# Other SBUF addresses for split weights and activations in a two-block transformer kernel on one core

## The chip, the core and the metric

One core of a Trainium2 chip runs the whole program. The metric is device time in microseconds of one execution. TensorE multiplies, VectorE and ScalarE do the elementwise work, and transfers from HBM are issued by SyncE's queue (SP). GpSimd sets a few tiles to zero.

## The reference

Two blocks follow each other on x of 256 tokens by 1,024 channels, all in float32. The first has two layers, each of a SwiGLU (1,024 to 2 x 2,816 to 1,024), a mixer and a second SwiGLU, with RMS norms and residuals around each; the mixer is a short convolution in the first layer and a gated delta rule with 16 heads in the second. The second block has sparse attention and an RWKV-7 recurrence side by side, merged by gates, and then a feed-forward with a convolution of width 3.

```python
def swiglu(x, w_gate_up, w_down):
    gate, up = jnp.split(x @ w_gate_up, 2, axis=-1)
    return (jax.nn.silu(gate) * up) @ w_down
...
for i in range(DEPTH):
    ff = swiglu(rms_norm(h, g[0]), ffn_w_gate_up[i, 0], ffn_w_down[i, 0])
    h = h + 0.5 * rms_norm(ff, g[1])
    ...  # mixer: h = h + rms_norm(mix, g[3])
    ff = swiglu(rms_norm(h, g[4]), ffn_w_gate_up[i, 1], ffn_w_down[i, 1])
    h = h + 0.5 * rms_norm(ff, g[5])
```

Nearly all the work lies in 19 products of x, or of a hidden activation, with a weight matrix (the list SEQUENCE).

## The kernel before

**Products in three terms.** Activations lie transposed, 128 channels on the partitions by 256 tokens, and a product takes weight tiles of 128 x 128 as TensorE's stationary operand. Both operands are split into a high part in TensorE's rounded format (fp32r) and the low part that remains. Each tile then takes three matmuls of 256 columns: high weight with high x, high weight with low x, low weight with high x (`mm3`, and `mm3s` for a product's first slices).

**The weight stream.** All weights lie in HBM as one stream of chunks, each of 128 partitions by four tiles (2,048 bytes to a partition). A chunk is loaded to one of six tiles wraw; ScalarE rounds it into one of seven tiles whi, VectorE subtracts that from wraw into one of seven tiles wlo (`split_next`), and the two are used for four tiles in turn (`next`). In the gated delta rule's input product a part of the chunks is split into a region arG instead (`borrow`).

**Operands.** The products up, sc_in, gdn_in, rw, nsa, merge, out2 and cup read the tiles xh and xl: the normed x, eight slices of 256 tokens. The products down, sc_out, gdn_out, proj and cdown read hidden activations in the regions a0, a1 and a2: slot k (of 256 columns) of these three in a row holds the high part of slice k, slot 22 + k its low part (`hidden`). The regions hold matrices of the two mixers in between. The profile writes whi, wlo, wraw and a for all buffers of a kind. In time, the products stand as up, down, sc_in, sc_out, up, down, up, down, gdn_in, gdn_out, up, down, rw, nsa, merge, proj, out2, cup, cdown; the third and fourth up run from about 470 and 920 us, and cup and cdown end the program.

**Addresses.** One pool places the tiles in the order in which they are made, each at the next multiple of 32 bytes of the partition. `fill` tiles hold nothing; they only move what follows. Worked out from the sizes, the tiles of the chunked products start at these remainders by 512 bytes; all slices and weight tiles within them are 512 or 1,024 bytes apart, so they keep the remainder:

| tile | before | changed |
|---|---|---|
| xh | 0 | 0 |
| xl | 0 | 16 |
| whi, seven buffers | 64 each | 32, 64, 96, 128, 160, 192, 224 |
| wlo, seven buffers | 64 each | 256, 288, 320, 352, 384, 416, 448 |
| a0 | 128 | 32 |
| a1 | 128 | 40 |
| a2 | 128 | 104 |
| arG | 128 | 128 |
| arM, fg, rb, acc, tmp, stm, x0 | 0 | 32 |

**The order of the work.** The program is made twice. In the first pass every instruction is recorded as a node with its engine, a price and what it depends on; a list scheduler (`ranks`, `schedule`) then sets an order for each engine, and the second pass issues the same instructions with that order (`arrange`). Dependences are kept by grains of 64 columns of a tile, counted from the tile's start:

```python
GRAIN = 64
...
cols = np.unique(cols // self.GRAIN).tolist()
```

Six times, at the start of a product whose x is made from the product before, `prepare` makes eight slices of h, xh and xl on VectorE and ScalarE while TensorE begins with slice 0.

Of the kernel before, what the change touches and what calls it, by code (L numbers as in the profile page):

```python
# [11 lines left out]
F32 = mybir.dt.float32  # L12
F32R = mybir.dt.float32r
# [6 lines left out]
P = 128  # L20
D = 1024
T = 256
KD = D // P
# [23 lines left out]
class Product:  # L47
# [4 lines left out]
    def __init__(self, name, index, kt, cols, groups=(), rows=None):  # L52
        rows = rows or [[(k * P, P)] for k in range(kt)]
        self.kt = kt
        self.cols = [c if isinstance(c, tuple) else (name, index, c, rows) for c in cols]
        self.groups = list(groups) + [1] * (len(cols) - sum(groups))
        self.order = []
        c = 0
        for n in self.groups:
            self.order += [(k, c + i) for k in range(kt) for i in range(n)]  # L60
            c += n
# [198 lines left out]
class Pace:  # L260
# [195 lines left out]
    def node(self, engine, op, out, ins, outs, price):  # L456
# [14 lines left out]
        for ap in [*ins, *outs]:  # L471
            tag = (getattr(ap.tensor, "tag", None) or "").split("_sb")[0]
            if tag in REGIONS:
                if self.current.get(tag) != ap.tensor.name:
# [145 lines left out]
class Streamer:  # L620


    def __init__(self, K, n_raw=6, n_split=7):
        self.K = K
        self.nc = K.nc
        pool = K.pool
        self.fill0 = pool.tile([P, 16], F32, name="fill2")
        self.raw = [pool.tile([P, CT * P], F32, name=f"wraw{i}") for i in range(n_raw)]
        self.hi = [pool.tile([P, ST * P], F32R, name=f"whi{i}") for i in range(n_split)]
        self.lo = [pool.tile([P, ST * P], F32R, name=f"wlo{i}") for i in range(n_split)]  # L630
        self.fill1 = pool.tile([P, 16], F32, name="fill3")
        self.order, self.place, self.at, self.ring = list(range(N_CHUNKS)), {}, {}, 0
        self.loaded = self.split = self.pos = 0

# [57 lines left out]


FILL = 24, 32
REGIONS = {"a0": 4096, "a1": 4096, "a2": 3072, "fg": 2048, "arG": 12288}


class Kernel:
    def __init__(self, nc, pool, psum, wstream, params, consts, xt, lowrank, w1, out):
        nc = self.nc = Engines(nc)  # L700
        self.pool = pool
        self.wstream, self.out, self.lowrank, self.w1 = wstream, out, lowrank, w1
        self.banks = [psum.tile([P, 512], F32, name=f"bank{i}") for i in range(8)]
        self.bank_at = 0
        self.side_at = 0
        self.par = pool.tile([P, N_PARAM], F32, name="par")
        self.eps = pool.tile([P, 1], F32, name="eps")
        self.half = pool.tile([P, 4, KD], F32, name="half")
        self.pad = [pool.tile([P, T + 3], F32, name=f"pad{i}") for i in range(5)]
        self.fill = [pool.tile([P, FILL[0]], F32, name="fill0")]  # L710
        self.con = pool.tile([P, N_CONST], F32, name="con")
        self.fill += [pool.tile([P, FILL[1]], F32, name="fill1")]
        self.h = pool.tile([P, KD, T], F32, name="h")
        self.xh = pool.tile([P, KD, T], F32R, name="xh")
        self.xl = pool.tile([P, KD, T], F32R, name="xl")
        self.regions = {}
        self.arM = pool.tile([P, 2048], F32, name="arM")
        self.fg = self.region("fg").rearrange("p (k t) -> p k t", t=T)
        self.rb = pool.tile([P, T], F32, name="rb")
        self.rb2 = pool.tile([P, T], F32, name="rb2")  # L720
        self.acc = pool.tile([P, T], F32, name="acc")
        self.tmp = [pool.tile([P, T], F32, name=f"tmp{i}") for i in range(8)]
        self.stm = [pool.tile([P, 512], F32, name=f"stm{i}") for i in range(4)]
        for t in self.pad:
            nc.vector.memset(t[:, :3], 0.0)
        self.fg0 = self.pad[4][:, 3:]
        self.x0 = [pool.tile([P, T], F32R, name=f"x0{i}") for i in range(2)]
        self.first = None
        self.tmp_at, self.tmp_n = 0, len(self.tmp)
        self.warm()  # L730
        self.table("natural_log_exp_and_others")
        self.W = Streamer(self)
        n = PCOLS["norm_g"][1]
        nc.pace.hurry = FIRST
        self.W.load_to(1)
        nc.sync.dma_start(self.par[:, :n], params[:, :n])
        nc.sync.dma_start(self.h[:, 0, :], xt[0:P, :])
        nc.pace.hurry = 0.0
        self.W.load_to(2)
        for i, (a, b) in enumerate(((1, 2), (2, 4), (4, 8))):  # L740
            nc.sync.dma_start(self.h[:, a:b, :], xt[a * P:b * P, :].rearrange("(k p) t -> p k t", p=P))
            self.W.load_to(3 + i)
        nc.sync.dma_start(self.con, consts)
        nc.sync.dma_start(self.par[:, n:], params[:, n:])
        nc.vector.memset(self.eps, EPS)
        for i, (l, j) in enumerate(((0, 1), (0, 5), (1, 1), (1, 5))):
            nc.vector.tensor_scalar(self.half[:, i], self.gain(l, j), 0.5, None, op0=ALU.mult)
# [11 lines left out]
    def region(self, tag, dtype=F32):  # L759

        n = self.regions[tag] = self.regions.get(tag, 0) + 1
        return self.pool.tile([P, REGIONS[tag]], dtype, name=f"{tag}_{n}", tag=tag)

    def hidden(self, **kept):

# [1458 lines left out]
```

## Time and profile before

| | us |
|---|---|
| median of 2 runs | 1554.49 (1554.04 to 1554.94) |
| profiled execution | 1564.22 |
| its span, first to last instruction | 1562.0 |
| TensorE matmuls busy (13,544 records) | 1545.8 |
| TensorE weight loads busy | 1495.5 |
| VectorE busy | 1199.4 |
| ScalarE busy | 1026.1 |

The times of the views are microseconds from the span's start. Every matmul has a weight load of its own, which overlaps the matmul before it. The records of matmuls overlap too (a record of 0.28 us, one every 0.11 us), so a sum of their times, or the mean of one, does not say how fast they follow each other; their count in a window does. The granted clock is TensorE's: 1.00 is 2.4 GHz, 0.50 is 1.2 GHz. A float32 matmul that is not fp32r appears as two records.

### The profile page before, as it was taken

The numbers are of one execution on the slowest core, as the hardware profiler recorded it, in microseconds if no ns is written. First come the engines' busy times: TensorE is split into PE (matmuls) and PEld (weight loads), VectorE is DVE, ScalarE is ACT, GpSimd is POOL, SyncE is SP. The second block draws the span as 40 slices with busy tenths as digits, with TensorE's granted clock in tenths as the row PEclk, the third lists the DMA queues.
The fourth block names the chain that finished last, engine by engine and source line by source line (L and its number), as shares of the span: only waits on it lengthen the run. The fifth ranks groups of instructions, "written<-read, shape, count | busy, mean of one in ns | idle before, by whom it ended". The sixth has DMA issues, their size and how long they took to land.

```text
span 1562.0 us, 35927 instructions
## 1 busy us (share of the span) xinstructions
PE 1545.8 (99%) x13544; PEld 1495.5 (96%) x13544; DVE 1199.4 (77%) x2527; ACT 1026.1 (66%) x2153; POOL 10.4 (1%) x24
## 2 busy tenths in 40 slices
PE   9999999999999999999999999999999999999999
PEld 9999999999999999989898899999997877999999
DVE  7776597887659777689897778775788866789973
ACT  7556566765657557678787866555683666578863
POOL 0000000000000000000000000000001000000000
PEclk9999999999999999999999999999998999999999
DMA  8666656566665667525342356666533322566664
GB/s 272 198 195 190 181 182 192 168 202 194 191 185 175 195 196 248 171 82 176 115 135 83 129 155 203 185 188 189 166 113 115 98 67 84 167 189 197 195 196 123
DMA packets 142670, 261.14 MB, mean 167 GB/s; under 512 B 15904, under 2 KB 17952, under 8 KB 142368
## 3 DMA queue, kind: packets, MB, share of 16 engines
q1 hardware_dynamic: 142496, 258.84, 55.5%
q8 instruction: 106, 1.74, 0.5%
q14 instruction: 68, 0.56, 0.1%
HBM read 257.73 MB, written 1.05 MB: 166 GB/s over the span
## 4 chain that ended last, share of the span: by engine, by line
PE 95%; ACT 2%; DVE 1%; issue 0%; DMA 0%; SPq 0%; DVEq 0%; ACTq 0%
PE bank L576 95%; ACT a L576 1%; ACT stm L576 1%; DVE a L576 0%; ACT arG L576 0%; ACT whi L576 0%; DVE fg L576 0%; DVE arG L576 0%; DMA h<-xt 0%; DVE wlo L576 0%; DVE xl L576 0%; DVE pad L576 0%; DVE tmp L576 0%; ACT pad L576 0%; ACT arM L576 0%
## 5 line engine op out<-in xcount | busy, mean ns | idle before, releaser
L576 ACT ACTIVATE whi<-wraw 128x512 fp32r<-128x512 f32 x956 | 599.2, 631 | 416.9 <-PE bank L576 311.8
L576 DVE TENSOR_TENSOR wlo<-wraw,whi 128x512 fp32r<-128x512 f32 x956 | 653.5, 689 | 274.8 <-ACT whi L576 268.6
L576 PE MATMUL bank<-xh,whi 128*128 128x256 f32 x2688 | 748.7, 283 | 5.7 <-DVE stm L576 3.6
L576 PE MATMUL bank<-xh,wlo 128*128 128x256 f32 x2688 | 746.8, 282 | 0.0
L576 PE MATMUL bank<-xl,whi 128*128 128x256 f32 x2688 | 740.7, 280 | 0.7 <-DVE xl L576 0.7
L576 PEld LDWEIGHTS bank<-xh,whi 128*128 128x128 f32 x2688 | 504.7, 189 | 14.6 <-issue 6.0
L576 PEld LDWEIGHTS bank<-xl,whi 128*128 128x128 f32 x2688 | 503.7, 189 | 8.1 <-issue 5.8
L576 PEld LDWEIGHTS bank<-xh,wlo 128*128 128x128 f32 x2688 | 502.7, 189 | 6.9 <-issue 5.9
L576 PE MATMUL bank<-a,whi 128*128 128x256 f32 x2272 | 403.8, 280 | 0.2
L576 PEld LDWEIGHTS bank<-a,whi 128*128 128x128 f32 x2272 | 347.1, 188 | 1.2 <-DVE a L576 0.5
L576 PE MATMUL bank<-a,wlo 128*128 128x256 f32 x1136 | 317.4, 279 | 0.0
L576 PEld LDWEIGHTS bank<-a,wlo 128*128 128x128 f32 x1136 | 212.7, 187 | 0.0
L576 DVE TENSOR_TENSOR tmp<-bank,rb 128x256 f32<-128x256 f32 x176 | 66.4, 419 | 6.6 <-ACT rb L576 1.4
L576 ACT ACTIVATE xh<-h,par 128x256 fp32r<-128x256 f32 x70 | 34.1, 499 | 12.7 <-DVE h L576 10.6
L576 ACT ACTIVATE arG<-bank 128x256 f32<-128x256 f32 (+2 forms) x87 | 37.8, 443 | 5.8 <-PE bank L576 5.5
L576 PE MATMUL bank<-a 64*128 64x256 f32 (+3 forms) x192 | 39.5, 380 | 1.5 <-DVE arG L576 1.5
L576 ACT ACTIVATE a<-tmp 128x256 fp32r<-128x256 f32 x88 | 35.8, 407 | 7.7 <-DVE tmp L576 7.6
L576 DVE TENSOR_TENSOR acc<-acc,tmp 128x256 f32<-128x256 f32 x92 | 38.6, 419 | 2.0 <-ACT acc L576 1.0
L576 DVE SCALAR_TENSOR_TENSOR arG<-arG,par 128x256 f32<-128x256 f32 x88 | 40.0, 477 | 0.0
L576 DVE TENSOR_TENSOR a<-tmp,a 128x256 fp32r<-128x256 f32 x88 | 36.8, 418 | 3.8 <-ACT a L576 3.8
L576 ACT ACTIVATE tmp<-tmp 128x256 f32<-128x256 f32 x88 | 35.4, 407 | 3.8 <-DVE tmp L576 3.7
L576 DVE TENSOR_TENSOR tmp<-tmp,tmp 128x256 f32<-128x256 f32 x88 | 36.7, 418 | 0.0
(253 smaller groups left out, 1226.1 us busy)
## 6 DMA issues: line engine op xcount, KB each, us to landing
wraw<-wstream SPq DMA_DIRECT2D x968, 256.0 KB, 2.9
arG<-cmp_w SPq DMA_DIRECT2D x1, 1024.0 KB, 4.8
out_dram<-h SPq DMA_DIRECT2D x8, 128.0 KB, 2.8
con<-consts SPq DMA_DIRECT2D x1, 734.0 KB, 5.4
h<-xt SPq DMA_DIRECT2D x1, 512.0 KB, 6.3
a<-lowrank SPq DMA_DIRECT2D x1, 512.0 KB, 4.1
par<-params SPq DMA_DIRECT2D x1, 283.5 KB, 4.7
h<-xt SPq DMA_DIRECT2D x2, 128.0 KB, 3.2
```

Of the source, the lines that this page charges most:

```text
L576: i = f(*args, **kw)
```

## The change

Each of the fourteen buffers whi and wlo is followed by a fill tile of eight elements (32 bytes), so the next one starts 32 bytes further by 512. The tile xl is made four elements longer, and its view begins at the fourth; likewise a view of region a1 begins at element 2 and of a2 at element 10 of a longer tile. The fill tile ahead of the raw weights goes. No instruction is added or taken away, and none has other operands than before but for their addresses.

```diff
--- before.py
+++ after.py
@@ -624,11 +624,17 @@
         self.K = K
         self.nc = K.nc
         pool = K.pool
-        self.fill0 = pool.tile([P, 16], F32, name="fill2")
         self.raw = [pool.tile([P, CT * P], F32, name=f"wraw{i}") for i in range(n_raw)]
-        self.hi = [pool.tile([P, ST * P], F32R, name=f"whi{i}") for i in range(n_split)]
-        self.lo = [pool.tile([P, ST * P], F32R, name=f"wlo{i}") for i in range(n_split)]
-        self.fill1 = pool.tile([P, 16], F32, name="fill3")
+        self.fills = []
+
+        def stepped(name):
+            t = pool.tile([P, ST * P], F32R, name=name)
+            self.fills.append(pool.tile([P, 8], F32, name=name + "f"))
+            return t
+
+        self.hi = [stepped(f"whi{i}") for i in range(n_split)]
+        self.lo = [stepped(f"wlo{i}") for i in range(n_split)]
+        self.fills.append(pool.tile([P, 16], F32, name="fill3"))
         self.order, self.place, self.at, self.ring = list(range(N_CHUNKS)), {}, {}, 0
         self.loaded = self.split = self.pos = 0
 
@@ -692,6 +698,8 @@
 
 
 FILL = 24, 32
+
+SHIFT = {"a1": 2, "a2": 10}
 REGIONS = {"a0": 4096, "a1": 4096, "a2": 3072, "fg": 2048, "arG": 12288}
 
 
@@ -712,7 +720,7 @@
         self.fill += [pool.tile([P, FILL[1]], F32, name="fill1")]
         self.h = pool.tile([P, KD, T], F32, name="h")
         self.xh = pool.tile([P, KD, T], F32R, name="xh")
-        self.xl = pool.tile([P, KD, T], F32R, name="xl")
+        self.xl = pool.tile([P, KD * T + 4], F32R, name="xl")[:, 4:].rearrange("p (k t) -> p k t", t=T)
         self.regions = {}
         self.arM = pool.tile([P, 2048], F32, name="arM")
         self.fg = self.region("fg").rearrange("p (k t) -> p k t", t=T)
@@ -759,7 +767,8 @@
     def region(self, tag, dtype=F32):
 
         n = self.regions[tag] = self.regions.get(tag, 0) + 1
-        return self.pool.tile([P, REGIONS[tag]], dtype, name=f"{tag}_{n}", tag=tag)
+        at = SHIFT.get(tag, 0)
+        return self.pool.tile([P, REGIONS[tag] + at], dtype, name=f"{tag}_{n}", tag=tag)[:, at:]
 
     def hidden(self, **kept):
```

Since the planner counts grains from the tile's start, the shifted views give it other dependences, and the orders that it sets differ in places. The first piece is VectorE's, at the start of sc_in, where prepare makes h, xh and xl anew (tmp holds the normed output of the product before, fg that output, rb the norm's factor). Before:

```order
L576 TENSOR_TENSOR h<-h,tmp_94 128x256
L576 TENSOR_TENSOR tmp_88<-fg_84,rb_86 128x256
L576 TENSOR_TENSOR tmp_90<-fg_84,rb_86 128x256
L576 TENSOR_TENSOR h<-h,tmp_88 128x256
L576 SCALAR_TENSOR_TENSOR xl<-h,par,xh 128x256
L576 TENSOR_TENSOR h<-h,tmp_90 128x256
L576 TENSOR_TENSOR tmp_92<-fg_84,rb_86 128x256
L576 SCALAR_TENSOR_TENSOR xl<-h,par,xh 128x256
```

and now:

```order
L576 TENSOR_TENSOR h<-h,tmp_94 128x256
L576 TENSOR_TENSOR x_106<-tmp_92,x_105 128x256
L576 TENSOR_TENSOR tmp_88<-fg_84,rb_86 128x256
L576 TENSOR_TENSOR tmp_93<-fg_84,rb_86 128x256
L576 SCALAR_TENSOR_TENSOR xl<-h,par,xh 128x256
L576 TENSOR_TENSOR h<-h,tmp_88 128x256
L576 TENSOR_TENSOR tmp_90<-fg_84,rb_86 128x256
L576 TENSOR_TENSOR h<-h,tmp_93 128x256
L576 TENSOR_TENSOR h<-h,tmp_90 128x256
L576 TENSOR_TENSOR tmp_92<-fg_84,rb_86 128x256
L576 SCALAR_TENSOR_TENSOR xl<-h,par,xh 128x256 x3
```

Before, the two rows of xl are slices 1 and 2. Now slice 1 stands where it stood, and the row "x3" holds slices 2, 0 and 3: slice 2 has moved behind two more operations, and slice 0 has come forward.

The second piece is TensorE's, in gdn_in, where matmuls of the delta rule's decays (a_5 is region a2, con a table of constants) stand among those of the stream. Before:

```order
L576 MATMUL bank_62<-xh,whi_127 128x256
L576 MATMUL bank_62<-xl,whi_127 128x256
L576 MATMUL bank_64<-a_5_7962,con 128x512
L576 MATMUL bank_62<-xh,wlo_134 128x256
L576 MATMUL bank_61<-xh,whi_127 128x256
```

and now:

```order
L576 MATMUL bank_62<-xh,whi_129 128x256
L576 MATMUL bank_62<-xl,whi_129 128x256
L576 MATMUL bank_62<-xh,wlo_143 128x256
L576 MATMUL bank_64<-a_5_7975,con 128x512
L576 MATMUL bank_61<-xh,whi_129 128x256
```

The matmul with con has moved behind one matmul of the stream. From here to the end of the delta rule, and again in the second block's mixers, TensorE's order differs by such moves; from the start to here, in the up and down products outside the mixers, and in cup and cdown it is the same.

## Rows read from the trace of the kernel before

**Rows 1.** The page, parts 1 and 2: busy time; granted TensorE clock by fortieths.
```profile
PE 1545.8 (99%) x13544; PEld 1495.5 (96%) x13544; DVE 1199.4 (77%) x2527; ACT 1026.1 (66%) x2153; POOL 10.4 (1%) x24
...
PEclk9999999999999999999999999999998999999999
```

**Rows 2.** The page, part 4: shares of the chain that ended last.
```profile
PE 95%; ACT 2%; DVE 1%; issue 0%; DMA 0%; SPq 0%; DVEq 0%; ACTq 0%
```

**Rows 3.** Groups of matmuls, whole span: count | busy, mean of one | idle before.
```profile
L576 PE MATMUL bank<-xh,whi 128*128 128x256 f32 x2688 | 748.7, 283 | 5.7 <-DVE stm L576 3.6 <-DVE pad L576 1.4 <-ACT xh L576 0.7
L576 PE MATMUL bank<-xh,wlo 128*128 128x256 f32 x2688 | 746.8, 282 | 0.0
L576 PE MATMUL bank<-xl,whi 128*128 128x256 f32 x2688 | 740.7, 280 | 0.7 <-DVE xl L576 0.7
L576 PE MATMUL bank<-a,whi 128*128 128x256 f32 x2272 | 403.8, 280 | 0.2
L576 PE MATMUL bank<-a,wlo 128*128 128x256 f32 x1136 | 317.4, 279 | 0.0
...
L576 PE MATMUL bank<-xh,arG 128*128 128x256 f32 x96 | 17.0, 287 | 0.0
...
L576 PE MATMUL bank<-xl,arG 128*128 128x256 f32 x48 | 11.9, 284 | 0.0
```

**Rows 4.** Windows, TensorE: length, busy (records), granted clock, DMA share, GB/s.
```profile
1400.00:1480.00 80.00, 80.00 (x709) 1.00 0.66 195
950.00:1010.00 60.00, 60.00 (x512) 1.00 0.64 190
1050.00:1100.00 50.00, 50.00 (x427) 1.00 0.64 187
1500.00:1555.00 55.00, 55.00 (x469) 1.00 0.56 167
660.00:668.00 8.00, 8.00 (x70) 1.00 0.01 2
```

**Rows 5.** Groups of matmuls from 1400 to 1460.
```profile
L576 PE MATMUL bank<-xh,whi 128*128 128x256 f32 x177 | 48.9, 276 | 0.0
```

**Rows 6.** Groups of matmuls from 950 to 1010.
```profile
L576 PE MATMUL bank<-xh,whi 128*128 128x256 f32 x170 | 47.8, 281 | 0.0
```

**Rows 7.** Groups of matmuls from 1500 to 1560.
```profile
L576 PE MATMUL bank<-a,whi 128*128 128x256 f32 x333 | 58.9, 280 | 0.0
```

**Rows 8.** Timeline, TensorE, after 845: start, length of the merged run.
```profile
845.28 1.95 PE L576 MATMUL bank<-arG,a 128*128 128x128 f32 x16
```

**Rows 9.** Groups of VectorE instructions, shapes apart.
```profile
L576 DVE SCALAR_TENSOR_TENSOR arG<-arG,par 128x256 f32<-128x256 f32 x88 | 40.0, 477 | 0.0
...
L576 DVE SCALAR_TENSOR_TENSOR arG<-pad,par,arG 128x256 f32<-128x256 f32 x16 | 7.6, 478 | 0.0
```

**Rows 10.** Waits of TensorE: total us, times, longest.
```profile
PE bank L576 <- DVE stm L576: 3.6, 1, 3.6
...
PE bank L576 <- DVE xl L576: 0.7, 2, 0.5
```

**Rows 11.** Windows of the three stretches at half clock, all engines.
```profile
771.50:778.40 6.90, 5.96 (x26) 5.81 (x27) 6.90 (x22) 4.58 (x11) 0.00 (x0) 0.51 0.37 115
1191.40:1201.60 10.20, 10.20 (x38) 7.88 (x36) 5.87 (x12) 2.66 (x5) 1.11 (x2) 0.50 0.08 26
1263.10:1266.50 3.40, 3.40 (x43) 2.83 (x44) 1.90 (x5) 3.34 (x9) 0.00 (x0) 0.50 0.23 77
```

**Rows 12.** Timeline, VectorE, start of the first sc_in product.
```profile
195.25 0.48 DVE L576 SCALAR_TENSOR_TENSOR xl<-h,par,xh 128x256 fp32r<-128x256 f32 x1
...
196.32 0.48 DVE L576 SCALAR_TENSOR_TENSOR xl<-h,par,xh 128x256 fp32r<-128x256 f32 x1
```

**Rows 13.** Timeline, TensorE, the same start.
```profile
196.56 0.84 PE L576 MATMUL bank<-xl,whi 128*128 128x256 f32 x6
...
197.36 0.28 PE L576 MATMUL bank<-xl,whi 128*128 128x256 f32 x1
```

## The prediction

> **What bounds the kernel now.** I began with the busy shares, the granted clock and the chain of waits. TensorE is busy in 99% of the span, its weight loads in 96%, and 95% of the chain that ended last is TensorE's own work [rows 1, 2]; VectorE (77%) and ScalarE (66%) have room. So the time is the number of matmuls times the step from one to the next, plus little else: the longest single wait of TensorE for another engine is 3.6 us [rows 10].
>
> Then the groups of matmuls: the chunked products issue 3 x 2,688 with xh or xl as the moving operand, 2,272 + 1,136 with a region a, and 96 + 48 with weights in arG [rows 3], 11,616 together. Their mean of 280 ns is no step, since they overlap; the step is a window's length over its count. A matmul record lasts 0.28 us and a window counts every record that touches it, so I add 0.28 us to the length. Last product with xh and xl: 80.28 us / 709 = **113.2 ns**. Last product with a: 55.28 / 469 = **117.9 ns**. The down product at 1050 to 1100: 50.28 / 427 = 117.8 ns [rows 4]. All at full clock, with TensorE busy throughout, and each window holds one kind of work [rows 5, 7]. So the same instruction, 256 columns against 128 x 128 weights, has two rates 4.5 ns apart, and what differs by the code is the address: xh and xl start at remainder 0 by 512 bytes, the a regions at 128, the weights of both at 64. But the window 950 to 1010 holds xh and xl again, at the addresses of 1400 to 1460 [rows 5, 6], and steps at 60.28 / 512 = 117.7 ns [rows 4]. So the address alone doesn't set the rate; a stretch can settle in either. With arG (weights at 128, moving operand at 0) the step is 8.28 / 70 = 118.3 ns [rows 4].
>
> By these, 3,408 matmuls with a, the 8 x 44 x 3 = 1,056 of the product around 950 and the 144 with arG run slow, 7,008 fast at best; the mean step is about 115.0 ns.
>
> **The change part by part.**
>
> *Remainders of the fourteen weight buffers, and shifts of xl, a1 and a2.* No matmul is added or removed, so the term is 11,616 times whatever the step changes by. The trace never shows these remainders: bounds are its nearest rows. Upward, the arG step of 118.3 ns for everything: 7,008 x 5.1 + 4,464 x 0.5 = 38 us lost. Downward, the shortest step of 128-column weights under a 256-cycle stream: sixteen fp32 matmuls with arG and a in 1.95 us, (1.95 - 0.28) / 15 = 111.3 ns [rows 8]; 11,616 x 3.7 = 43 us gained. Those read half as many moving bytes, so I take them as an end and not as the value. In between lies the fast rate of this very work. I take: the matmuls with a go from 117.8 to 113.2 ns, since what all their windows share is the distance between their one remainder and the weights' one remainder, and after the change there is no such fixed distance; 3,408 x 4.5 = **15.3 us gained**. The product around 950 stays as it is (4.8 us more if it too turns fast), arG stays (its own tile keeps remainder 128; 0.7 us).
>
> The Trainium skill has a rule against the shifts: its page SBUF — State Buffer, section Specifications (TRN2), gives lines of 16 bytes and a penalty for each crossing. A row of 1,024 bytes at 8 modulo 16 touches 65 lines where it touched 64; as an estimate from that page, 1/64 of a step, 1.8 ns on at most 3,408 matmuls, 6 us lost. No row here has such a moving operand in the chunked products.
>
> *VectorE and ScalarE on shifted tiles.* Nothing: a SCALAR_TENSOR_TENSOR that reads a pad at an offset of a few elements takes 478 ns, one with aligned operands 477 [rows 9], and neither engine is the bound.
>
> *The planner's order.* It tracks dependences in grains of 64 elements, so a 256-element slice shifted by 4, 2 or 10 elements touches five grains and shares one with its neighbour. Hence the pieces of order shown. At the six starts where x is made anew, xl of slice 2 waits behind two more VectorE operations. Before, it began at 196.32 [rows 12] for a matmul at 197.36 [rows 13]; xl takes 0.48 us, so the slack is 0.56 us. Two operations later at 0.33 us each it is late by 0.1 us; with the semaphore 0.2 us, and six starts give **1.2 us lost**. Slice 3 has 2 us more and is in time. The weight splits put back there by the same move, nine operations or some 3 us, lie behind a ring of seven buffers of 12 matmuls each, 9.5 us; if that cover were gone, the move would cost those 3 us a start. SP's order swaps a few neighbouring loads, which the ring hides too.
>
> In the delta-rule and attention stretches some hundreds of matmuls change places with a neighbour or a few, at 0.1 us each. That can move a wait or one of three stretches at half clock: 20.5 us, in which TensorE is busy for 19.6 us [rows 11], so they cost up to 9.8 us now. If order cured them, 10 us are gained; a fourth like the longest would lose 5 us. I take 0.
>
> **Sum.** The profiled execution took 1564.2 us (span 1562.0, the rest around it); -15.3 + 1.2 = -14.1 us makes it 1550. The median of the runs is 1554.5, 0.6% less, so the forecast is 1554.5 - 14.1 = **1540 us**. With the product around 950 and arG fast too it is 1535; the order's ends take these to 1525 and 1545, and if a third of the matmuls with a stay slow, to 1550.
>
> **The rivals.**
>
> *No contention by address.* The Trainium skill, page TensorE: Matmul & The Clock Gate, section Step-by-step: what each phase is for, says that weight loads and the moving operand come through two independent ports, and that loading the next weights takes nothing from a running matmul. As a mechanism here: the two rates are only states left by what ran before, and the layout is without effect. For it: the slow product at the fast product's addresses [rows 5, 6]. Against it: the matmuls with a are slow in both windows of them [rows 4]. Time: 1554.5 + 1.2 = 1556. Chance 0.12.
>
> *Better than the fast rate.* The fast rate itself holds some interference between the two reads, and spread remainders remove it. For it: the 111.3 ns of the fp32 matmuls [rows 8]. Against it: 113.2 ns is held in both early and late products, as a floor would be. At 111.3 ns throughout, 1554.5 - 43 + 1 = 1512. The first page's back-to-back formula, N / 2.4 + 2.5, would give 109.2 ns; as an estimate, 1488. This decides (over 2% faster) once the mean step is under 112.3 ns. Chance 0.29.
>
> *Slower: the fast stretches are lost.* The products with xh and xl run fast at one fixed pair of remainders, 0 against 64. Now the pair changes every four weight tiles, half of the weight buffers start at an odd multiple of 32 bytes, xl at 16, a1 and a2 at 8, and the stream settles where arG's did. For it: arG, the one other distance in the trace, is the slowest of all, and one whole product fell slow at the good pair. Against it: nothing in the trace shows a cost of a start within 64 bytes. With all at 117.8 ns: 7,008 x 4.5 = 32 us, 1587; with all at 118.3, 1594. It decides from a mean step of 117.7 ns. Chance 0.17.
>
> **How the numbers follow.** About 2% (31 us) can be told from no change here. The forecast has 0.42, all of it within 2%, and so has the rival without effect, 0.12: same 0.54. Faster 0.29, slower 0.17. The range goes from 1500, which leaves out the third of the second rival that comes nearest to a full cure (0.09), to 1588, which leaves out the half of the last above it (0.08). The likeliest case's own range is 1525 to 1550.
>
> **What would show it.** Count over length again. Right: windows of the down products at 113 to 114 ns (some 488 matmuls in 55 us where 469 stood), xh and xl unchanged. No contention: 117.8 with a, as now. Better: any window of a chunked product under 112 ns. Slower: windows with xh and xl at 117 ns or more. The order's step is right if TensorE's waits for VectorE's xl grow to about 1 us and no more; it is wrong if the half-clock stretches change by over 5 us. The forecast is wrong if the rates within one window mix by buffer, which no row of before can show.

## The result, and the profile after

The changed kernel takes 1601.8 us (median of 2 runs, 1601.1 to 1602.5) where the kernel before took 1554.5 on the same chip: 1.028 times as long, with a 95% interval of 1.023 to 1.033. It is slower. The forecast was 1540 us, the range 1500 to 1588; both missed.

The changed kernel's profile, busy time, answers to [rows 1]:

```profile
PE 1581.5 (99%) x13544; PEld 1529.3 (96%) x13544; DVE 1202.2 (75%) x2527; ACT 1026.1 (64%) x2153; POOL 10.3 (1%) x24
```

TensorE is still busy for 99% of the span, with as many instructions as before. It is busy 35.7 us longer, and the span is 38.6 us longer (1600.6). VectorE worked 2.8 us longer, ScalarE as long as before. So the same matmuls took longer; TensorE's idle time, span less busy, only went from 16.2 to 19.1 us. (The chain of waits is no help here: walked back from the end it stops after 10% of the span.)

Its groups of matmuls, as in [rows 3] (count | busy, mean of one | idle before), say where:

```profile
L576 PE MATMUL bank<-xh,whi 128*128 128x256 f32 x2688 | 754.1, 284 | 6.2 <-DVE pad L576 2.7 <-DVE tmp L576 2.0 <-ACT xh L576 1.0
L576 PE MATMUL bank<-xh,wlo 128*128 128x256 f32 x2688 | 752.5, 284 | 0.0
L576 PE MATMUL bank<-xl,whi 128*128 128x256 f32 x2688 | 751.5, 284 | 1.0 <-DVE xl L576 1.0
L576 PE MATMUL bank<-a,whi 128*128 128x256 f32 x2272 | 409.2, 282 | 0.2
L576 PE MATMUL bank<-a,wlo 128*128 128x256 f32 x1136 | 320.5, 282 | 0.0
```

Every group is busy 3 to 11 us longer, and the idle times hardly differ. Since the records overlap, the steps have to come from windows. These answer to [rows 4] (length, TensorE busy and records, granted clock, DMA share, GB/s): two windows with xh and xl, the second in the product that ran slow before, the last down product with a, and the stretch with arG:

```profile
40.00:120.00 80.00, 80.00 (x681) 1.00 0.66 188
...
980.00:1040.00 60.00, 60.00 (x512) 1.00 0.66 190
...
1540.00:1595.00 55.00, 55.00 (x464) 1.00 0.57 166
675.00:683.00 8.00, 8.00 (x70) 1.00 0.10 33
```

With the formula of the prediction, (length + 0.28 us) / count (one record more or less changes a step from 80 us by 0.2 ns, one from 11 us by 1.2 and one from 8 us by 1.7): xh and xl 117.9 and 117.7 ns, where the fast window had 113.2 and the slow one 117.7; a 119.1 ns, where it had 117.9; arG 118.3 as before. Put into the counts: 7,008 x 4.7 = 33 us for the matmuls that ran fast (at best: 279 more with xh and xl, at 803 to 820 and 1124 to 1142 us, ran slow before too, 1.3 us less), nothing for the 1,056 that ran slow already, 3,408 x 1.2 = 4 us for a. That is 36 to 37 of the 38.3 us between the two profiled executions (1602.5 and 1564.2). The medians lie 47 us apart, since the timed runs of before were 10 us shorter than its profiled one. What made those 10 us is not shown; two things that differ from run to run are: which of two steps a product falls into (e3, e12), and how long TensorE is at half clock (e6, e7, e11).

### The profile page after: what moved, and what is told of

Same layout as the page of the kernel before. It is cut to its first block, busy times and chain, and to the rows that moved or that the text cites. A ratio compares the mean times of both kernels' runs of the same rounds, so it can differ in the third digit from the quotient of the medians.

```text
span 1600.6 us, 35925 instructions
## 1 busy us (share of the span) xinstructions
PE 1581.5 (99%) x13544; PEld 1529.3 (96%) x13544; DVE 1202.2 (75%) x2527; ACT 1026.1 (64%) x2153; POOL 10.3 (1%) x24
## 5 line engine op out<-in xcount | busy, mean ns | idle before, releaser
L576 PE MATMUL bank<-xl,whi 128*128 128x256 f32 x2688 | 751.5, 284 | 1.0 <-DVE xl L576 1.0
L576 PE MATMUL bank<-a,whi 128*128 128x256 f32 x2272 | 409.2, 282 | 0.2
L576 PEld LDWEIGHTS bank<-a,whi 128*128 128x128 f32 x2272 | 351.3, 189 | 0.8 <-DVE a L576 0.5
```

The source lines that it names most:

```text
L576: i = f(*args, **kw)
```

## The experiments

Three theories. **P**, the pair: which remainders the moving operand and the weights have against each other sets TensorE's step; the kernel before had one good pair in every xh and xl matmul, and the change takes it away. **S**, the shifts: rows of xl, a1 and a2 that begin off a multiple of 64 (or 16) bytes cost by themselves. **O**, the order: the planner's altered order costs. From e5 on, P is put as **D**: what counts is the distance by 512 bytes between the two operands, the moving operand's start less the weights' start (before, xh and xl had 0 - 64 = -64, a had 128 - 64 = +64).

### e1 to e3: the change in three parts

e1, the weights' part alone (against the changed kernel; xl, a1 and a2 unshifted, a fill and a tail keep the other tiles in place):

```
-SHIFT = {"a1": 2, "a2": 10}
+SHIFT = {}
-        self.xl = pool.tile([P, KD * T + 4], F32R, name="xl")[:, 4:].rearrange("p (k t) -> p k t", t=T)
+        self.xl = pool.tile([P, KD, T], F32R, name="xl")
```

> The weights' part of the change alone: fourteen buffers of split weights stepped by 32 bytes (32 to 448), xl at 0 and a0, a1, a2 all at 32 without shifts. Theory P (the pair decides: one fixed pair of remainders, moving operand 0 and weights 64, lets TensorE lock into its 113.3 ns step, and a pair that changes from weight to weight never locks): the xh and xl products lose the fast step by this part alone, mean step 117.5 to 118.3 ns, time 1585 to 1602 us. Theory S (the shifts by 16, 8 and 72 bytes cost, because rows then begin off a multiple of 64 bytes): xh, xl and a products here at or under 113.5 ns or as before, time 1540 to 1558 us. Theory O (the altered order of instructions costs): this kernel has the order of before, so 1550 to 1560 us.

e2, the shifts alone (against before; fills keep the weights at 64 and a0 at 128):

```
+SHIFT = {"a1": 2, "a2": 10}
-        self.xl = pool.tile([P, KD, T], F32R, name="xl")
+        self.xl = pool.tile([P, KD * T + 4], F32R, name="xl")[:, 4:].rearrange("p (k t) -> p k t", t=T)
```

> The shifts alone: all weights at 64 as before, xl at 16, a1 8 and a2 72 bytes beyond a0's remainder of 128, and the instruction order of the changed kernel. Theory P: three fixed distances with long stretches of the same pair, so xh keeps 113.3 ns; xl may be fast or slow but is constant within a product; a as before, 117.8: 1550 to 1575 us. Theory S: xl and a products at 119 ns as in the changed kernel: xl 2,336 matmuls by +4 to +6 ns is +9 to +14 us, a 3,400 by +1.5 ns is +5 us, and VectorE's and ScalarE's passes late behind them: 1568 to 1602 us. Theory O: 1560 to 1570 us, with xh at 113.3.

e3, the changed kernel's order on the addresses of before: the planner counts its grains as if xl, a1 and a2 were shifted.

```
             p0, c0 = divmod(ap.offset, pitch)
+            c0 += next((v for k, v in {"xl": 4, "a1": 2, "a2": 10}.items() if name == k or name.startswith(k + "_")), 0)
```

> The instruction order of the changed kernel on the addresses of before, to the byte. Theory P and theory S: 1552 to 1560 us, with xh and xl at 113.3 ns. Theory O: 1575 us or more, with PE's step unchanged and longer waits on VectorE.

Measured against before on the same chip: e1 1600.8 us, 1.026 times (1.021 to 1.031); e2 1593.1, 1.021 (1.016 to 1.027); e3 1569.3, 1.004 (1.001 to 1.007). Before itself ran from 1555.1 to 1571.3 there.

Windows of e1, of e2 (each time a product with xh and xl, 40 to 120) and of e3 (two products with xh and xl), columns as above:

```profile
40.00:120.00 80.00, 80.00 (x674) 1.00 0.66 186
```
```profile
40.00:120.00 80.00, 80.00 (x686) 1.00 0.66 190
```
```profile
60.00:120.00 60.00, 60.00 (x511) 1.00 0.64 186
...
980.00:1040.00 60.00, 60.00 (x532) 1.00 0.69 194
```

e1 steps at 119.1 ns and e2 at 117.0. So the weights' part alone, as P expected, takes the whole loss (at a step a little over P's 118.3) and the shifts alone most of it, and they don't add: there is one fast step to lose, and both lose it. O falls as the cause: e3 has the new order and loses 0.4%, 5.6 us (0.9 to 10 by the interval; its 1569 us lie above what P and S gave, as do most runs of before beside it). Its windows hold the two old rates at the old addresses, 118.0 and 113.3 ns, and now it is the product at 980 that is fast and the first that is slow; which one a product falls into changed between these two executions. (The expectation of e2 counts 2,336 matmuls with xl; [rows 3] has 2,688.) P's number for e2 was wrong: it gave xh, whose own pair is unchanged there, 113.3 ns. The matmuls go round in threes (xh with whi, xl with whi, xh with wlo), and with xl moved every third one has another distance. S as the cause of the loss falls with e1, which has no shift and the whole loss; whether a shift costs anything by itself e2 can't tell, and e9 has to.

### e4 and e5: one distance for all

e4 is before with a0, a1 and a2 moved from 128 to 0, so that the down products have xh's distance; a tail behind a2 keeps arG at 128.

```
-        self.fill1 = pool.tile([P, 16], F32, name="fill3")
+        self.fill1 = pool.tile([P, 112], F32, name="fill3")
```

> Before with one move: regions a0, a1 and a2 from remainder 128 to 0, so that the down product reads its moving operand at the remainder that x has in the fast products (0 against weights at 64); arG stays at 128. Theory P: the 3,400 matmuls with a go from 117.8 to 113.3 ns, -15 us: 1537 to 1543 us. If it is not the pair of remainders but something else of those products (their moving operand is freshly written, their output goes to other banks) that makes them slow: 1552 to 1558 us with the down windows at 117.8 as before.

e5 is e4 with everything from h on 32 bytes further:

```
-FILL = 24, 32
+FILL = 24, 40
```

> The kernel with a at remainder 0 once more, with every tile from h on moved by 32 bytes: xh, xl and a at 32, weights at 96, arG at 160. Theory D (what counts is the distance from the moving operand to the weights, here -64 as in the fast products): 113.3 ns throughout, 1540 to 1548 us. Theory A (each remainder by itself counts: a tile must begin on a multiple of 64 bytes): step 116 ns or more in all products, 1575 to 1605 us.

e4: 1543.4 us, 0.989 times before (0.985 to 0.994), 0.4 us over its range. e5: 1547.4, 0.991 (0.988 to 0.995). Windows of e4 (the first product, the one around 960, the last down product) and of e5 (the first product):

```profile
40.00:120.00 80.00, 80.00 (x708) 1.00 0.68 197
...
960.00:1020.00 60.00, 60.00 (x532) 1.00 0.68 194
...
1490.00:1535.00 45.00, 45.00 (x400) 1.00 0.60 170
```
```profile
60.00:120.00 60.00, 60.00 (x532) 1.00 0.70 195
```

All at 113.2 to 113.4 ns, the down products too: 3,408 x 4.7 = 16 us, and 4.6 us from the product around 960 that was fast this time, make all but 0.2 of the 20.8 us between the two profiled executions (1564.2 and 1543.4). e5 has the same step at 32 and 96 in place of 0 and 64: the distance counts, and a start off 64 bytes does no harm. Not every matmul of e5 is fast, though: by the starts of its records, the first 150 or so of the products at 194, 285, 469 and 917 us follow each other at 117.8 ns, at the same distance (see e12).

### e6 to e8: other distances, held fixed

Each is before with the weights at another remainder, a left at 128. Only the fills before and behind the weight buffers differ (e8 shown):

```
-        self.fill0 = pool.tile([P, 16], F32, name="fill2")
+        self.fill0 = pool.tile([P, 8], F32, name="fill2")
-        self.fill1 = pool.tile([P, 16], F32, name="fill3")
+        self.fill1 = pool.tile([P, 24], F32, name="fill3")
```

> Before with all weights at remainder 0 in place of 64: x at 0 (distance 0), a at 128 (distance 128). Theory D: one steady step for each product kind, with no mix inside a window. Of its size nothing is known for these two distances: 113.3 or less for xh and xl would give 1540 to 1556 us, 117.8 for all of them 1587 us, 119 for all 1600 us. If any steady pair is fast, 1540 to 1556 us.

> Before with all weights at remainder 256: x at 0 (distance -256), a at 128 (distance -128). Theory D as for weights at 0: one steady step for each product kind; 1540 to 1600 us by its size. If any steady pair is fast, 1540 to 1556 us. If only the distance -64 is fast, 1587 us or more.

> Before with all weights at remainder 32, the first remainder that the changed kernel gives a weight buffer: x at 0 (distance -32), a at 128 (distance 96). In the changed kernel matmuls with x at 0 and the weights at 32 took 118.6 ns on average among other pairs. Theory D with a lock for every steady pair: 113.3 ns for xh and xl, 1540 to 1556 us. If the remainder 32 itself is slow: 118 to 119 ns, 1590 to 1605 us.

1613.7 us (1.031, 1.028 to 1.034), 1607.2 (1.027, 1.023 to 1.031) and 1604.5 (1.025, 1.021 to 1.029). Windows of e6, e7, e8, each with xh and xl first, then a:

```profile
40.00:120.00 80.00, 80.00 (x669) 1.00 0.64 184
1560.00:1600.00 40.00, 40.00 (x339) 1.00 0.59 176
```
```profile
40.00:120.00 80.00, 80.00 (x669) 1.00 0.66 185
1560.00:1595.00 35.00, 35.00 (x297) 1.00 0.52 146
```
```profile
40.00:120.00 80.00, 80.00 (x678) 1.00 0.68 188
1560.00:1600.00 40.00, 40.00 (x336) 1.00 0.51 148
```

Distance 0: 120.0 ns; +128: 118.8; -256: 120.0; -128: 118.8; -32: 118.4; +96: 119.9. So a fixed pair is not enough, and the hope for a better distance than -64 fails at all six; e6 lies above every time given for it. e6 and e7 have the same two steps, yet their profiled executions took 1614.4 and 1603.8 us: in e6 TensorE's granted clock is 0.50 for 34.1 us in the two mixers, in e7 for 6.8. Equal steps can't make that difference; the half-clock time can. The first remainder that the change gives a weight buffer is one of the slow ones.

### e9: TensorE by itself

The network is left out. 54 stretches of 120 matmuls each (its expectation miscounts them as 51), with operands in SBUF and no other engine at work; all tiles begin at 128, so its remainders are distances. The inner loop:

```
nc.tensor.matmul(to, wh, xh, start=i == 0, stop=False)
nc.tensor.matmul(to, wh, xl, start=False, stop=False)
nc.tensor.matmul(to, wl, xh, start=False, stop=i == TRIPLES - 1)
```

> TensorE by itself (it leaves the whole network out and copies x through): 51 stretches of 120 matmuls (128x128 fp32r weights, 128x256 moving) in the triples of the products, with no VectorE, ScalarE or DMA work beside them and about 1 us between stretches. The first 32 stretches hold one fixed distance from moving operand to weights each, 0 to 496 bytes in steps of 16; then the same distances at other absolute remainders, distances off 16 bytes, a second remainder for x's low part or for the low weights, and weights that step from buffer to buffer. Theory D (the distance by 512 bytes sets a steady step, whatever runs on the other engines): 120.0 ns at 0, 118.7 at 128 and 384, 118.3 at 480, 117.8 at 64, 113.3 or 117.8 at 448, the same at other absolute remainders; with a second pair in the triple every third matmul, 116 to 119 ns even where the first pair alone takes 113.3. Theory C (contention with the other engines' reads and writes makes the difference): one step for all distances, 113.3 ns or less.

Windows of 11 us, one within each stretch, so the step is 11.28 us / count. In order: distances 0, 32, 64, 96, 112, 128, 192, 224, 256, 448 (the old -64); 440; 8; 72; then 448 with xl 16 further, with xl 256 further, and last with the weights stepped as the change steps them:

```profile
15.10:26.10 11.00, 11.00 (x94) 1.00 0.01 1
45.40:56.40 11.00, 11.00 (x96) 1.00 0.01 1
75.30:86.30 11.00, 11.00 (x96) 1.00 0.01 1
105.20:116.20 11.00, 11.00 (x94) 1.00 0.01 1
120.40:131.40 11.00, 11.00 (x100) 1.00 0.01 1
134.80:145.80 11.00, 11.00 (x95) 1.00 0.01 1
...
195.00:206.00 11.00, 11.00 (x99) 1.00 0.00 0
224.50:235.50 11.00, 11.00 (x96) 1.00 0.00 0
254.30:265.30 11.00, 11.00 (x94) 1.00 0.01 1
...
433.90:444.90 11.00, 11.00 (x100) 1.00 0.00 0
...
537.00:548.00 11.00, 11.00 (x94) 1.00 0.01 1
582.30:593.30 11.00, 11.00 (x96) 1.00 0.01 1
...
597.20:608.20 11.00, 11.00 (x93) 1.00 0.01 1
...
612.60:623.60 11.00, 11.00 (x96) 1.00 0.01 1
672.30:683.30 11.00, 11.00 (x99) 1.00 0.00 0
...
804.80:815.80 11.00, 11.00 (x95) 1.00 0.01 1
```

The steps of the whole kernels come back with nothing beside TensorE: 94 records are 120.0 ns, 95 are 118.7, 96 are 117.5, 99 to 100 are 112.8 to 113.9 (by the starts of the records all of these last take 113.3). So contention with the other engines is not needed for the effect (theory C falls). Of S this much is left: a moving operand 8 bytes off a 16-byte boundary runs at 117.5 ns at distance 8, faster than the aligned one at 0, but at 72 at 121.3 ns, the slowest of all 54 stretches, where the aligned neighbours 64 and 80 take 117.8 and 118.3 by their starts. A surcharge of one size does not show; a cost at single distances isn't excluded. Of all 16 multiples of 32 bytes only 192 and 448 are fast, which are 256 apart; 0 and 256 agree as well. The other fast distances are 112 and 368, off 32 bytes and again 256 apart. Not every pair 256 apart agrees: by their starts 16 and 272 take 118.7 and 116.7 ns, 160 and 416 118.7 and 117.3. The eight steps of 0 to 224 average 118.0 ns (160 had 95 records too), and the stretch stepped as in the change, with xl unshifted, has 118.7 (e1, the same in the whole kernel: 119.1). The changed kernel's 117.7 and 117.9 for xh and xl are near what an even mix of distances gives. With xl 16 further, 117.5 ns against the 117.0 of e2's products.

### e10 and e11: the best layout, and where a second remainder is free

e10 is e4 with arG moved from 128 to 64; e11 is e4 with a fill of 64 elements between the high and the low weight buffers (and 64 less behind them):

```
-TAIL = {"a2": 32}
+TAIL = {"a2": 16}
```
```
+        self.fill2 = pool.tile([P, 64], F32, name="fill4")
         self.lo = [pool.tile([P, ST * P], F32R, name=f"wlo{i}") for i in range(n_split)]
```

> The kernel with a at remainder 0, and arG moved as well, from 128 to 64, so that the 154 matmuls that read x against weights in arG stand at distance -64 too (they took 118.7 ns). All fp32r matmuls at one distance: 113.3 ns, the 154 save 154 x 5.4 ns = 0.8 us over the run with a alone moved (1543.4): 1538 to 1548 us, 0.985 to 0.992 of the time of before. If the distance isn't what matters there: 1543 us.

> The kernel with a at 0, with the low weights moved from 64 to 320 and the high weights left at 64: two remainders that lie 256 bytes apart, in every triple of matmuls. Theory D256 (the distance counts by 256 bytes, as in the stretches of TensorE by itself, where this mix took 113.3 ns): 113.3 ns throughout, 1540 to 1550 us. Theory D512 (only one pair of remainders by 512 bytes can hold the fast step): every third matmul at another pair, 116.5 to 119 ns, 1575 to 1605 us.

e10: 1544.0 us, 0.987 (0.984 to 0.990; the ratio leaves out one of its six executions, which took 1570.2 us), not to be told from e4; the 0.8 us (its expectation counts 154 matmuls, [rows 3] has 144) are below what the time shows. e11: 1552.6, 0.992 (0.989 to 0.996). Windows of e11, the first product and the last down product:

```profile
40.00:120.00 80.00, 80.00 (x709) 1.00 0.67 196
1490.00:1535.00 45.00, 45.00 (x400) 1.00 0.66 199
```

113.2 ns in both, with two remainders in every three matmuls: D256 holds for this pair, D512 falls. Its median is 2.6 us above the 1550 expected. For the profiled execution, 7.7 us longer than that of e4, the traces show where: TensorE is at half clock for 20.5 us in the second block's mixers of e11, in e4 for 3.4 us, after which the clock is full again (windows of e11 first, then e4):

```profile
1245.30:1265.80 20.50, 20.50 (x206) 0.50 0.09 31
```
```profile
1249.10:1266.00 16.90, 16.90 (x279) 1.00 0.06 18
```

e4 and e10 beat both kernels, by 1.1 and 1.3% of before.

### e12: the two states of one distance

Once more TensorE with the network left out, at -64 and its neighbours. As in e9, with other stretches and, for a part of them, splits of weights and DMA loads:

```
for _ in range(8):
    s += [(64, 20, True), (448, 30, False)]
s += [(448, 20, True)] * 8
...
LOADED = [(448, 20, True)] * 10 + [(64, 20, True), (448, 30, False)] * 6
```

(distance, threes of matmuls, whether a wait stands before the stretch.)

> TensorE by itself once more (the network left out), to see what decides between 113.3 and 117.8 ns at the distance -64 that the runs of before show: stretches at -64 behind a wait, straight behind stretches at 64 (117.8 ns) and at 0 and -32, with a new bank every 24 matmuls, and then the same with splits of weights on ScalarE and VectorE and their DMA loads beside them. Theory H (history: a stretch at -64 that follows one of 117.8 ns without a wait keeps that step): the stretches behind 64 stay at 117.8, those behind a wait take 113.3. Theory L (load: what the other engines read and write at the start decides): 113.3 in all stretches without load, a part of them at 117.8 with it. If all are at 113.3, neither is shown and the choice stays open.

It was built otherwise than meant: the scheduler put most of the splits and loads beside the first stretches, up to about 115 us, and the rest at 395 to 480, and pulled a few matmuls ahead of each wait. Windows, in order: +64 with load; without load +64 behind a wait, -64 straight behind it, -64 behind a wait, distance 0, -64 straight behind that, -64 straight behind -32 twice; and -64 behind a wait with load:

```profile
14.00:20.00 6.00, 6.00 (x55) 1.00 0.84 266
```
```profile
136.00:142.00 6.00, 6.00 (x53) 1.00 0.01 3
143.00:151.00 8.00, 8.00 (x70) 1.00 0.00 0
179.20:185.20 6.00, 6.00 (x56) 1.00 0.01 3
263.50:268.50 5.00, 5.00 (x44) 1.00 0.00 0
271.00:279.00 8.00, 8.00 (x73) 1.00 0.01 2
...
333.00:341.50 8.50, 8.50 (x75) 1.00 0.00 0
...
368.50:377.00 8.50, 8.50 (x77) 1.00 0.00 0
...
427.80:433.40 5.60, 5.60 (x50) 1.00 0.39 140
```

Without load: 118.5 ns, then -64 at 118.3 behind it; behind a wait 112.1 (of 56 records, each worth 2 ns); distance 0 at 120.0 and -64 behind it 113.4; behind -32 117.1 and 114.0 (by the starts 117.8 in three such stretches and 113.3 in the fourth). So theory H holds there as far as 117.8 goes: -64 has two steady steps, 113.3 and 117.8, and one that comes straight from a 117.8 stretch keeps it, in all eight such stretches without load; behind -32 either comes up. With load both come up where they did not before: +64 at 114.2 ns, -64 at 117.6 behind a wait. L is so far right that load changes the draw. What decides each single draw in the whole kernel stays open. Nor is it shown that these draws make the times of before spread over 16 us on one chip (1555.1 to 1571.3): e5 and e11, whose products stand at -64 or 256 bytes from it, spread as widely (14.5 and 15.5 us), and the half-clock stretches differ from run to run too.

## Why the prediction was wrong

**What bounds the kernel** was right: TensorE's step times the count, and all of the loss is in the step.

**The matmuls with a from 117.8 to 113.2 ns, and xh and xl unchanged (15.3 us gained)**: this is the step that failed, in sign. It took 113.2 for the undisturbed rate and the one fixed distance of a for a disturbance that ends when there is no fixed distance. It is the other way round: most distances cost 117 to 120 ns (e6 to e9), -64 is one of the few good ones, and before had it in every xh and xl matmul. Taking the fixed distance away cost those matmuls 4.7 ns and gave a 1.2 ns more instead of 4.5 less. The mix shows in the window, too: by the starts of the records from 36 us on, twelve at a time, the steps of after go 116.5, 117.9, 118.0, 118.2, 118.3, 118.6, 118.0 ns and round again, with the seven buffers; rates that mix by buffer are what the prediction itself named as the sign of being wrong. Of what the prediction read, one thing was right: a was slow at its distance, and setting it to xh's gives the forecast gain (e4, 16 us where 15.3 were expected). +64 can hold the fast step as well (e12, under load), but no down product of before or e3 did.

**The penalty of the 16-byte lines** (an estimate of 6 us) isn't seen. The Trainium skill, page SBUF — State Buffer, section Specifications (TRN2), speaks of a penalty for each crossing. In e9 the distance 8 runs at 117.5 ns and 440 at 120.0, both 8 off a line, within the aligned distances' 113.3 to 120.0, and 72 at 121.3, above them; a surcharge of 1.8 ns everywhere doesn't show, and the measurement decides. For a as a whole the shifts cost next to nothing: by the starts of the records the long down products take 118.8 to 118.9 ns in e1, without shifts, and 119.1 to 119.3 in after.

**VectorE and ScalarE at nothing**: right. The arG of [rows 9] is not a shifted tile; the group that writes xl is (before, then after):

```profile
L576 DVE SCALAR_TENSOR_TENSOR xl<-h,par,xh 128x256 fp32r<-128x256 f32 x70 | 33.0, 479 | 1.5 <-ACT xh L576 1.5
```
```profile
L576 DVE SCALAR_TENSOR_TENSOR xl<-h,par,xh 128x256 fp32r<-128x256 f32 x70 | 32.2, 476 | 0.6 <-ACT xh L576 0.6
```

VectorE's group a<-tmp,a takes 419 ns (418 before), its wlo<-wraw,whi 688 (689), and ScalarE's a<-tmp 407 (407).

**The order, 1.2 us, half-clock stretches within 5 us**: small, as forecast, by the prediction's own signs; the second sign was met by luck. TensorE's waits for xl in the profile after, total, times and longest, against [rows 10], and its three half-clock stretches behind the start against [rows 11]:

```profile
PE bank L576 <- DVE xl L576: 1.0, 2, 0.7
```
```profile
854.20:867.80 13.60, 13.60 (x138) 0.50 0.37 117
891.70:895.10 3.40, 3.40 (x18) 0.51 0.00 0
1164.80:1168.20 3.40, 3.15 (x15) 0.50 0.51 169
```

The waits for xl grew by 0.3 us, from 0.7 to 1.0. By the starts of the records, the first 36 matmuls of five such products lose 0.06 to 0.11 us each in after, and 0.24 to 0.32 us each in e3, which has the same order at the fast step; the forecast was 0.2 us a start. The half-clock time is 20.4 us after 20.5, but none of the three stretches is where it was, and with the order of before it is 34.1 us in e6 and 6.8 in e7: the sum says nothing of the order. The wait on stm of 3.6 us is gone and others took its place.

**The rivals.** "Slower: the fast stretches are lost" came true in its own rows: arG's 118.3 ns, the one other distance in the trace, was the best sign of what other distances would do. It was given 0.17, because nothing in the trace showed a cost of a start within 64 bytes. That was no evidence against it: the loss comes from the distance, which the trace did show at two values besides -64 (a and arG), both slow. Its mechanism was only half right: starts at an odd multiple of 32 bytes do no harm of themselves (e5), and without the shifts of xl, a1 and a2 the loss is the same (e1). "No contention by address" fell. The Trainium skill, page TensorE: Matmul & The Clock Gate, section Step-by-step: what each phase is for, says that weights and moving operand come through two independent read ports and that a load takes nothing from a running matmul; by e9, with TensorE alone, the same instructions take 113 to 121 ns by their distance alone. How the reads meet inside is not shown here. "Better than the fast rate" fell too: no distance in e6 to e9 had a step under that of -64.

## What to carry to other kernels

Where every matmul loads new weights, put the moving operand and the weights at one distance by 256 bytes for all of them, high and low parts alike, and measure that distance: here -64 took 113.3 ns in most stretches and most others 117 to 120, an estimated 3 to 5% of the whole time (11,616 matmuls at 4 to 6.7 ns). When two windows of the same instruction differ in rate, ask first what the fast one has that the slow one lacks, before calling the slow one disturbed. A few stretches of the instruction by itself, one distance each, answer in one run what a layout tried on the whole kernel answers one value at a time.

## What the runs showed of the hardware that I had not expected

- The step of a 128x128 fp32r weight load with a 256-column matmul depends on the distance of the two operands in SBUF: 120.0 ns at 0 and 256, 113.3 (112.8 to 113.9 by the windows) at 192, 448 and 112, with no other engine at work (e9).
- One distance can hold two steps, 113.3 and 117.8 ns, and one of -64 that follows a 117.8 stretch without a wait kept it (e12, without load: 118.3 ns behind +64, 113.4 behind distance 0).
- Moving xl alone by 16 bytes slows the xh matmuls between which it stands as well (e2: 117.0 ns over all three; by the starts 115.0, 118.4 and 117.8 ns from xh with whi, xl with whi and xh with wlo to the next).
- Executions with the same instructions and order differ by how long TensorE is at half clock: 20.5 us from 1245 us on in e11, where e4 has 3.4, and 34.1 us in all in e6, where e7 has 6.8.
